# Reordering four token mixers and the cover beside the last one, in a one-core hybrid encoder layer

## The chip, the core and the metric

The kernel runs on one core of one Trainium2 chip. The metric is the device time of the whole program in microseconds (us): the median of three runs. Beside it one execution is profiled, and its instructions, waits and transfers are what this document reads.

## The reference, cut to what matters

One layer of a streaming encoder for 1024 prompt rows and 64 sample rows, width 1024, all in float32:

```python
p = x @ w_in + b_in                       # columns split among four mixers
y = [mLSTM(p), attention(p), HGRN2(p), RG_LRU(p)]     # A, B, C, D, each (t, 512)
mix = sum(sigmoid(x @ w_mg[m] + b_mg[m]) * (y[m] @ w_br[m]) for m in range(4))
x1 = layer_norm(ALPHA * x + mix @ w_out)
x2 = layer_norm(ALPHA * x1 + (gelu(causal_dwconv3(x1 @ w_ff_gate)) * (x1 @ w_ff_up)) @ w_ff_down)
```

The attention needs one forget value per head and row (`log_sigmoid`, then a running sum over the cache and the new rows); the mLSTM needs two gate values per head and row and a running maximum. These are 16 columns of `w_in` in all, the gate rows. The four mixers do not depend on each other: they may run in any order. The states, keys, values and forget logs of both groups are outputs too.

## The kernel before, in words

**Numbers.** A float32 operand is split into a rounded high part and a rest, and a product is three matmuls (high by high, high by rest, rest by high; `mm3`, L305). A weight tile of 128 output columns is loaded by SP (L263), its high part is made by GpSimd for `w_in` (L271) and by ScalarE for all else (L273), its rest by VectorE (L274). `plan` (L199 to L252) lists all weight tiles in the order of use; `wget` issues loads two tiles ahead of use, into two raw and three split buffers.

**Dense tiles.** `dense` (L323) makes one tile of 128 output columns over 1088 rows in three steps (384, 384 and 320 rows), 24 matmuls each. A step is the unit of cover that is woven beside other work. The gate tiles `sigmoid(x @ w_mg)` are stored to DRAM (`th_d`) and read back when the branches are merged. Most of them are made in pairs (`gate_pair`, L503, by `pair`, L373): two tiles with seven products in place of eight over 768 of the rows, fed by sums of weight blocks (`wsums`, L281) and of x blocks (`xsums`, L334). The tiles listed in `PLAIN` (L32) are plain dense tiles: four at the start, while x is being transposed, and tiles 6 and 7 of mixer 0 near the end.

**Order.** The program is written as generators, and `weave(a, na, b, nb)` (L435) runs two of them step by step in the ratio na:nb. `P_X(u)` makes the dense tiles of unit u of mixer X, `M_X(u)` the mixer's own small work (transposes, small matmuls, scans, exponentials). A planner then places the instructions on each engine: work that it takes to be ready may move ahead of work written earlier that is not, by its own estimate of durations; each engine executes its list strictly in that order. DMAs are issued by SP, likewise in order.

The order is D (RG-LRU, 4 units of 6 dense steps), C (HGRN, 4 of 12), B (attention, 4 of 9), A (mLSTM, 2 of 18):

1. Start: `xload`, the bias loads (`pload`, L460; `b_mg`, `ff_conv_w`, `ff_conv_b` and the convolution state go to one tile `pk2r`), transposes of x (`xsplit`), the plain gate tiles of mixer 3. The biases are turned by one transpose (L485), copied (L486), and `bhalf` made from it (L488).
2. 13 gate pairs (L494 to L496).
3. `gate_rows` (L599): 16 columns by a small matmul (L616, L617), through DRAM (`zr_d`, `ls_d`) into a layout with all partitions for the logarithm.
4. `P_D(0)`; then M_D(u) beside P_D(u+1). `fox_rows` (L632: load `ls_d` and the cache's logs, running sums on VectorE, transposes L644 and L657) is chained behind M_D(1); `ml_rows` (L668) behind M_D(3), beside P_C(0).
5. M_C(u) beside P_C(u+1); M_C(3) beside 7 steps of P_B(0), the other 2 steps beside the two tails that M_C leaves (`until_flushed`, L1487).
6. M_B(u) beside P_B(u+1); M_B(3) beside the 18 steps of P_A(0).
7. M_A(0) beside P_A(1). M_A(1) beside 14 steps of a chain: gate tiles 6 and 7 of mixer 0 (6 dense steps), in whose last three steps `ysplit(3, c)` puts the first mixer's result in the place of x; then `merge(3, (0, 2))`, 12 steps of 12 matmuls. Its last four steps stand beside the four tails.
8. `ysplit` of the other mixers and the merges (L766), the output projection, the FFN.

Of the kernel before, what the change touches and what calls it, by code (L numbers as in the profile page):

```python
# [15 lines left out]
OP = mybir.AluOpType  # L16
# [4 lines left out]
P = 128  # L21
# [7 lines left out]
TINY = 1e-30  # L29
ALPHA = 2.0 ** 0.25  # L30
NSLOT = 19
PLAIN = ((3, 0), (3, 2), (0, 6))  # L32
TGRP = ((0, 1, 2), (3, 4, 5), (8, 6, 7))

ML_Q, ML_K, ML_V, ML_O, ML_I, ML_F = 0, 256, 512, 1024, 1536, 1540
# [15 lines left out]
PK_MG = 0  # L51
PK_FW = 32
PK_FB = 80
# [17 lines left out]
def trunk_kernel(ctx: ExitStack, tc: tile.TileContext, I, O, dbg=None):  # L71
# [17 lines left out]
    def phase(s):  # L89
        if temps[0] is not None:  # L90
            temps[0].close()
        temps[0] = ExitStack()
        temps[1] = temps[0].enter_context(tc.tile_pool(name="sp" + s, bufs=3, reuse_waits="tile"))
# [28 lines left out]
    def bank(tag, n=512):  # L122
        return ps1.tile([P, n], F32, tag=tag, name=nm("ps" + tag))
# [80 lines left out]
    def plan_in(c0):  # L204
        plan.append((("in", c0), win(c0), 8))

    def plan_mg(m, e):
        for g in (e, e + 1):
            plan.append((("mg", m, g), I["w_mg"][0, m, :, g * P:g * P + P].rearrange("(k p) c -> p k c", p=P), 8))
# [10 lines left out]
        for c0 in (RG_X, RG_G):  # L220
            plan_in(c0 + u * P)
    for u in range(4):
        for c0 in (HG_F, HG_Q, HG_I, HG_G):
            plan_in(c0 + u * P)
    for u in range(4):
        for c0 in (FX_K, FX_Q, FX_V):
            plan_in(c0 + u * P)
    for u in range(2):
        for c0 in (ML_K + u * P, ML_Q + u * P, ML_V + 2 * u * P, ML_V + 2 * u * P + P,
                   ML_O + 2 * u * P, ML_O + 2 * u * P + P):  # L230
            plan_in(c0)
    plan_mg(0, 6)
    for m in (3, 2, 1, 0):
        for e in (0, 2, 4, 6):
# [191 lines left out]
    def run(*gens):  # L426
        for g in gens:
            for _ in g:
                pass

    def chain(*gens):
        for g in gens:
            yield from g

    def weave(a, na, b, nb):  # L435

        live = [True, True]
        done = [0, 0]
        while live[0] or live[1]:
            i = 0 if live[0] and (not live[1] or done[0] * nb <= done[1] * na) else 1  # L440
            try:
                next((a, b)[i])
                done[i] += 1
            except StopIteration:
                live[i] = False
# [9 lines left out]
    def xload(*tts):  # L455
        for tt in tts:
            xt[tt] = wide["x"].tile([P, D], F32, tag=f"x{tt}", name=nm("xt"), bufs=1) if tt < 8 else slot([P, D], F32, "xt")
            pinned(SP.dma_start(xt[tt][0:tw(tt)], xsrc(tt)))

    def pload(dst, src, raw):  # L460
        n = src.shape[0] // P
        pinned(SP.dma_start(raw[dst:dst + n, :], src.rearrange("(r p) -> r p", p=P)))
# [3 lines left out]
    wissue(0, True)  # L466
    xload(1, 2)
    wissue(1, True)
    for dst, src in ((PK_MG, I["b_mg"][0].rearrange("a b -> (a b)")),
                     (PK_FW, I["ff_conv_w"][0].rearrange("a b -> (a b)")), (PK_FB, I["ff_conv_b"][0]),  # L470
                     (PK1B, I["state_ffn_conv"][0, 0].rearrange("a b -> (a b)"))):
        pload(dst, src, pk2r)
    xload(3, 4, 5, 6, 7, 8)
    for dst, src in ((0, I["b_in"][0, 0:1536]), (12, I["b_in"][0, 1544:3080]), (24, I["b_in"][0, 3088:6160])):
        pload(dst, src, pkb)
    for dst, src in (
# [4 lines left out]
        pload(dst - PK_NG, src, pkr)  # L481
    for tt in range(3):
        xsplit(xt[tt], tt, tt % 2 == 0)
    pt = bank("s", 1024)
    PE.transpose(pt[:, 512:512 + PK2], pk2r[0:PK2, :], ident)  # L485
    V.tensor_copy(pk2, pt[:, 512:512 + PK2])  # L486
    bhalf = const([P, 32], "bhalf")
    V.tensor_scalar(bhalf, pk2[:, PK_MG:PK_MG + 32], 0.5, None, OP.mult)  # L488

    th_d = [[dp.tile([P, T], F32, name=f"th_d{m}_{e}") for e in range(8)] for m in range(4)]  # L490

# [44 lines left out]
    n = PK1 - PK_NG  # L536
    PE.transpose(pt[:, PK_NG:PK1], pkr[0:n, :], ident[0:n, 0:n])
    V.tensor_copy(pk[:, PK_NG:PK1], pt[:, PK_NG:PK1])

    def bc(c0):  # L540
        return pk[:, bcol(c0):bcol(c0) + 1]
# [266 lines left out]
    def P_D(u):  # L808
        xp = slot([P, TP + TS + 6], F32, "xp")
        V.memset(xp[:, 0:3], 0.0)  # L810
        V.tensor_copy(xp[:, TP + 3:TP + 6], pk[:, PK_SC + u:PK_SC + 12:4])
        b = bc(RG_X + u * P)

        def ev(c, n0, n, ps):
            n1 = min(n, TP - n0)
            S.activation(xp[:, 3 + n0:3 + n0 + n1], ps[:, 0:n1], AF.Identity, bias=b)
            if n1 < n:
                S.activation(xp[:, TP + 6:TP + 6 + TS], ps[:, n1:n], AF.Identity, bias=b)
        dx = dense(("in", RG_X + u * P), ev)
        gg = slot(s="gg")  # L820
        bg = bc(RG_G + u * P)

        def ev2(c, n0, n, ps):
            S.activation(gg[:, n0:n0 + n], ps, AF.Identity, bias=bg)
        dg = dense(("in", RG_G + u * P), ev2)
        if u:
            yield from dx
        else:
            for _ in range(2):
                next(dx)  # L830
                yield
                next(dg)
                yield
            next(dx)
            yield
        if u == 0:
            prep_rg()
        uc = slot(s="uc")
        for o, n, _, a in SEG:
            V.tensor_scalar(uc[:, o:o + n], xp[:, a:a + n], pk[:, PK_CW + u:PK_CW + u + 1],  # L840
                            pk[:, PK_CB + u:PK_CB + u + 1], OP.mult, OP.add)
            for j in range(1, 4):
                V.scalar_tensor_tensor(uc[:, o:o + n], xp[:, a + j:a + j + n],
                                       pk[:, PK_CW + 4 * j + u:PK_CW + 4 * j + u + 1],
                                       uc[:, o:o + n], OP.mult, OP.add)
        V.tensor_copy(stD[:, 2:5, u], xp[:, TP:TP + 3])
        V.tensor_copy(stD[:, 5:8, u], xp[:, T + 3:T + 6])
        if u:
            next(dg)
            yield  # L850
        uh = slot(dt=F32R, s="uh")
        S.activation(uh, uc, AF.Copy)
        ul = slot(dt=F32R, s="ul")
        V.tensor_sub(ul, uc, uh.bitcast(F32))
        yield from dg
        st["D", u] = uc, uh, ul, gg

    def M_D(u):
        uc, uh, ul, gg = st.pop(("D", u))
        gates = []  # L860
        for gi, pb in ((0, PK_BA), (1, PK_BX)):
            gt = slot(s="gt")
            for c, (n0, n) in enumerate(CH):
                ps = bank("m")
                mm3(ps[:, :n], [(wab["h"][:, u, gi, :], wab["l"][:, u, gi, :], uh[:, n0:n0 + n], ul[:, n0:n0 + n])])
                S.activation(gt[:, n0:n0 + n], ps[:, :n], AF.Sigmoid, bias=pk[:, pb + u:pb + u + 1])
                yield
            gates.append(gt)
        r, ig = gates
        V.tensor_tensor(ig, ig, uc, OP.mult)  # L870
        tn = slot(s="tn")
        S.activation(tn, r, AF.Tanh, scale=p8[:, u:u + 1])
        S.activation(gg, gg, AF.Gelu_apprx_tanh)
        a = r
        S.activation(a, r, AF.Exp, scale=m8[:, u:u + 1])
        yield
        e2 = slot(s="e2")
        S.activation(e2, a, AF.Square)
        V.scalar_tensor_tensor(e2, e2, 1.0, tn, OP.add, OP.mult)
        V.tensor_scalar(e2, e2, 0.0, None, OP.max)  # L880
        S.activation(e2, e2, AF.Sqrt)
        V.tensor_tensor(e2, e2, ig, OP.mult)
        yield
        h = slot(s="h")
        V.tensor_tensor_scan(h[:, 0:TP], a[:, 0:TP], e2[:, 0:TP], 0.0, OP.mult, OP.add)
        V.tensor_tensor_scan(h[:, TP:T], a[:, TP:T], e2[:, TP:T], pk[:, PK_H0 + u:PK_H0 + u + 1], OP.mult, OP.add)
        V.tensor_copy(stD[:, 0:2, u], h[:, TP - 1:T:TS])
        G.tensor_tensor(gg, h, gg, OP.mult)
        yput(3, u, gg)
        yield  # L890
# [606 lines left out]
    slot_pool(NSLOT)  # L1497
    phase("D")
    gate_rows()
    run(P_D(0))  # L1500
    weave(M_D(0), 10, P_D(1), 6)
    weave(chain(M_D(1), fox_rows()), 13, P_D(2), 6)
    weave(M_D(2), 10, P_D(3), 6)
    weave(chain(M_D(3), ml_rows()), 17, P_C(0), 12)
    out_D()
    phase("C")
    for u in range(1, 4):
        weave(M_C(u - 1), 19, P_C(u), 12)
    g = P_B(0)
    weave(M_C(3), 19, islice(g, 7), 7)  # L1510
    until_flushed(g)
    phase("B")
    for u in range(1, 4):
        weave(M_B(u - 1), 23, P_B(u), 9)
    weave(M_B(3), 23, P_A(0), 18)
    phase("A")
    weave(M_A(0), 21, P_A(1), 18)

    def last_gates():
        for i, _ in enumerate(gates(0, (6, 7))):  # L1520
            if i >= 3:
                xtiles("y", (i - 3,))
                ysplit(3, i - 3)
            yield

    g = chain(last_gates(), merge(3, (0, 2)))
    weave(M_A(1), 21, islice(g, 14), 14)
    until_flushed(g)
    for c in range(3):
        ysplit(2, c)  # L1530
    run(merge(3, (4, 6)))
    for c in range(3):
        ysplit(1, c)
    run(merge(2, (0, 2, 4, 6)))
# [324 lines left out]
```

## Time and profile before

| | us |
|---|---|
| median of 3 runs (lowest, highest) | 2154.87 (2153.61, 2157.75) |
| the profiled execution's own time | 2155.62 |
| span in its profile, first to last instruction | 2153.9 |
| TensorE matmul busy | 2095.9 |
| VectorE busy | 1283.2 |
| ScalarE busy | 791.9 |
| mean granted TensorE clock | 0.991 |

Matmuls are pipelined, so their busy time is not their work; idle time of TensorE and stretches at a lower granted clock are the places to look at. PE is TensorE's matmuls, PEld its weight loads, DVE VectorE, ACT ScalarE, POOL GpSimd, SP SyncE. "A <- B" means that A's engine sat idle until B ended.

### The profile page before, as it was taken

What the parts mean: (1) busy time and instruction counts of PE and PEld (TensorE: products, weight loads), DVE (VectorE), ACT (ScalarE), POOL (GpSimd) and SP (SyncE); (2) the same over time, 40 slices, a digit from 0 to 9 for tenths busy, and PEclk for the clock granted to TensorE, in tenths of its full rate; (3) what the DMA queues carried; (4) which work ended last, traced back from release to release, by engine and by line L of the source; (5) the groups of instructions that cost most, each with busy time, mean ns of one, the idle gap of its engine ahead of it and who ended that gap; (6) DMA issues with size and microseconds to landing.
All of it is one profiled execution on the core that took longest, in us unless ns stands there. A gap on an engine that the chain in (4) does not pass through costs nothing.

```text
span 2153.9 us, 32071 instructions
## 1 busy us (share of the span) xinstructions
PE 2095.9 (97%) x12879; PEld 1939.7 (90%) x12879; DVE 1283.2 (60%) x2438; ACT 791.9 (37%) x1352; POOL 223.9 (10%) x232
## 2 busy tenths in 40 slices
PE   8999999989999999999999999999999999999998
PEld 7999999989988878888999988999889999998886
DVE  6544442556666667556442466767369776666656
ACT  4433332555454424344332342213134333334341
POOL 0000000111211132212101100000130000000112
PEclk9999999999999999999999999999999999999999
DMA  5233233112111122132131156345221223237652
GB/s 165 81 101 102 95 107 97 44 54 62 38 47 44 39 90 65 59 99 81 51 81 41 52 198 175 125 143 179 93 84 51 80 72 89 66 99 280 215 200 103
DMA packets 199856, 212.56 MB, mean 99 GB/s; under 512 B 15324, under 2 KB 170792, under 8 KB 199708
## 3 DMA queue, kind: packets, MB, share of 16 engines
q1 hardware_dynamic: 199708, 210.52, 31.2%
q8 instruction: 101, 1.65, 0.3%
q14 instruction: 47, 0.39, 0.1%
HBM read 160.93 MB, written 49.56 MB: 98 GB/s over the span
## 4 chain that ended last, share of the span: by engine, by line
PE 46%; DVE 3%; DMA 1%; issue 0%; POOL 0%; ACT 0%; DVEq 0%; SPq 0%; ACTq 0%; POOLq 0%
PE pss L386 8%; PE pss L1769 5%; PE psd L308 4%; PE psd L310 4%; PE psd L309 4%; PE psm L308 3%; PE psm L310 3%; PE psm L309 3%; PE psd L1769 2%; PE psm L1769 2%; PE pss L308 1%; PE pss L310 1%; PE pss L309 1%; PE psm L386 1%; PE psm L1385 1%; PE psm L1172 0%
## 5 line engine op out<-in xcount | busy, mean ns | idle before, releaser
L308 PE MATMUL psd<-xh,wh 128*128 128x384 f32 (+1 forms) x1504 | 504.7, 336 | 3.0 <-ACT xh L182 2.6
L310 PE MATMUL psd<-xh,wl 128*128 128x384 f32 (+1 forms) x1504 | 494.2, 329 | 0.0
L309 PE MATMUL psd<-xl,wh 128*128 128x384 f32 (+1 forms) x1504 | 493.5, 328 | 0.4 <-DVE xl L183 0.4
L274 DVE TENSOR_TENSOR wl<-wr,wh 128x1024 fp32r<-128x1024 f32 x179 | 224.3, 1256 | 236.5 <-ACT wh L273 168.4
L308 PEld LDWEIGHTS psd<-xh,wh 128*128 128x128 f32 x1504 | 286.4, 190 | 9.9 <-issue 3.4
L309 PEld LDWEIGHTS psd<-xl,wh 128*128 128x128 f32 x1504 | 285.0, 189 | 1.9 <-DVE xl L183 0.9
L310 PEld LDWEIGHTS psd<-xh,wl 128*128 128x128 f32 x1504 | 285.0, 189 | 0.4
L273 ACT ACTIVATE wh<-wr 128x1024 fp32r<-128x1024 f32 x131 | 138.7, 1059 | 361.1 <-PE psd L309 96.3
L386 PE MATMUL pss<-xs,sh 128*128 128x384 f32 x536 | 136.9, 336 | 0.0
L308 PE MATMUL psm<-yh,wh 128*128 128x384 f32 (+1 forms) x384 | 128.6, 335 | 6.9 <-DVE we L1394 2.7
L271 POOL TENSOR_SCALAR wh<-wr 128x1024 fp32r<-128x1024 f32 x48 | 53.3, 1110 | 770.1 <-PE pss L386 346.1
L309 PE MATMUL psm<-yl,wh 128*128 128x384 f32 (+1 forms) x384 | 127.2, 331 | 0.0
L310 PE MATMUL psm<-yh,wl 128*128 128x384 f32 (+1 forms) x384 | 127.1, 331 | 0.0
L297 DVE TENSOR_TENSOR sl<-st,sh 128x1024 fp32r<-128x1024 f32 x54 | 66.1, 1224 | 51.9 <-ACT sh L296 51.5
L386 PEld LDWEIGHTS pss<-xs,sh 128*128 128x128 f32 x536 | 96.1, 188 | 0.1
L296 ACT ACTIVATE sh<-st 128x1024 fp32r<-128x1024 f32 x54 | 57.3, 1061 | 97.1 <-PE pss L386 44.6
L386 PE MATMUL pss<-xs,sl 128*128 128x384 f32 x268 | 90.0, 336 | 0.0
L1572 POOL TENSOR_TENSOR lrs<-lrs,mhalf 128x1 f32<-128x1 f32 (+1 forms) x16 | 9.8, 614 | 755.9 <-ACT hh L1716 423.9
L1235 DVE CUSTOM_DVE_ANT_0 Pt<-pss,fcb 128x128 f32<-128x128 f32 (+7 forms) x64 | 48.1, 753 | 65.1 <-PE pss L1230 64.6
L308 PE MATMUL psd<-x1h,wh 128*128 128x320 f32 (+1 forms) x272 | 85.3, 313 | 0.6 <-DVE x1l L193 0.6
L310 PE MATMUL psd<-x1h,wl 128*128 128x320 f32 (+1 forms) x272 | 84.9, 312 | 0.0
L309 PE MATMUL psd<-x1l,wh 128*128 128x320 f32 (+1 forms) x272 | 84.8, 312 | 0.0
(556 smaller groups left out, 4530.1 us busy)
## 6 DMA issues: line engine op xcount, KB each, us to landing
wr<-in_w_in_dram SPq DMA_DIRECT2D x48, 512.0 KB
wr<-in_w_ff_down_dram SPq DMA_DIRECT2D x48, 512.0 KB
th_d<-th SPq DMA_DIRECT2D x32, 544.0 KB
th<-th_d SPq DMA_DIRECT2D x32, 544.0 KB
wr<-in_w_mg_dram SPq DMA_DIRECT2D x32, 512.0 KB
wr<-in_w_br_dram SPq DMA_DIRECT2D x16, 512.0 KB
wr<-in_w_ff_gate_dram SPq DMA_DIRECT2D x16, 512.0 KB
wr<-in_w_ff_up_dram SPq DMA_DIRECT2D x16, 512.0 KB
```

Of the source, the lines that this page charges most:

```text
L271: G.tensor_scalar(h, raw, 1.0, 1.0, OP.mult, OP.mult)
L273: S.activation(h, raw, AF.Copy)
L274: V.tensor_sub(l, raw, h.bitcast(F32))
L296: S.activation(h, t, AF.Copy)
L297: V.tensor_sub(l, t, h.bitcast(F32))
L308: PE.matmul(ps, wh, mh, start=i == 0, stop=False)
L309: PE.matmul(ps, wh, ml, start=False, stop=False)
L310: PE.matmul(ps, wl, mh, start=False, stop=i == n - 1)
L386: PE.matmul(ps, w[:, k, :], x[:, k, :], start=start and k == 0 and i == 0, stop=k == 3 and i == 2, skip_group_check=not start)
L1235: V.tensor_tensor_reduce(Pt[:, 0:L].rearrange("p (b n) -> p b n", b=nb), ps.rearrange("p (b n) -> p b n", b=2)[:, 0:nb, 0:n], cbs[hh][:, 0 ...
L1385: PE.matmul(ps[0:w, 0:w], kt[r, t0:t0 + w], qt[r, t0:t0 + w], start=True, stop=True)
L1769: PE.matmul(ps[hf], a[:, f % 8, o:o + P], w[:, 0, sl], start=f == 0 and i == 0, stop=f == 15 and i == (2 if tt < 8 else 1))
```

## The change

The mixers run in the order D, B, C, A. The gate tiles 4 and 5 of mixer 0 leave the pairs (12 pairs are left) and become plain tiles at the end: beside M_A(1) stand 8 steps of four plain gate tiles, the other 4 steps beside the four tails, and the whole of `merge(3, ...)` comes after them. The first part of `fox_rows` (two loads and a running sum) is issued directly behind `gate_rows`, and the rest is woven with P_D(0) after its first two steps; the loads of `ml_rows` are issued before M_B(3), and the rest is chained behind M_B(3), beside P_C(0). M_D(3) stands beside P_B(0), M_C(3) beside 14 steps of P_A(0). At the start `b_mg` is loaded alone into a tile of 32 rows ahead of the later x tiles and turned alone; the three other vectors are loaded behind x and turned later, before the pairs.

```diff
@@ -29,7 +29,7 @@
 TINY = 1e-30
 ALPHA = 2.0 ** 0.25
 NSLOT = 19
-PLAIN = ((3, 0), (3, 2), (0, 6))
+PLAIN = ((3, 0), (3, 2), (0, 4), (0, 6))
 TGRP = ((0, 1, 2), (3, 4, 5), (8, 6, 7))
 
 ML_Q, ML_K, ML_V, ML_O, ML_I, ML_F = 0, 256, 512, 1024, 1536, 1540
@@ -220,15 +220,16 @@
         for c0 in (RG_X, RG_G):
             plan_in(c0 + u * P)
     for u in range(4):
-        for c0 in (HG_F, HG_Q, HG_I, HG_G):
+        for c0 in (FX_K, FX_Q, FX_V):
             plan_in(c0 + u * P)
     for u in range(4):
-        for c0 in (FX_K, FX_Q, FX_V):
+        for c0 in (HG_F, HG_Q, HG_I, HG_G):
             plan_in(c0 + u * P)
     for u in range(2):
         for c0 in (ML_K + u * P, ML_Q + u * P, ML_V + 2 * u * P, ML_V + 2 * u * P + P,
                    ML_O + 2 * u * P, ML_O + 2 * u * P + P):
             plan_in(c0)
+    plan_mg(0, 4)
     plan_mg(0, 6)
     for m in (3, 2, 1, 0):
         for e in (0, 2, 4, 6):
@@ -466,11 +467,12 @@
     wissue(0, True)
     xload(1, 2)
     wissue(1, True)
-    for dst, src in ((PK_MG, I["b_mg"][0].rearrange("a b -> (a b)")),
-                     (PK_FW, I["ff_conv_w"][0].rearrange("a b -> (a b)")), (PK_FB, I["ff_conv_b"][0]),
+    pkm = small([32, P], "trif", 1)
+    pload(0, I["b_mg"][0].rearrange("a b -> (a b)"), pkm)
+    xload(3, 4, 5, 6, 7, 8)
+    for dst, src in ((PK_FW, I["ff_conv_w"][0].rearrange("a b -> (a b)")), (PK_FB, I["ff_conv_b"][0]),
                      (PK1B, I["state_ffn_conv"][0, 0].rearrange("a b -> (a b)"))):
-        pload(dst, src, pk2r)
-    xload(3, 4, 5, 6, 7, 8)
+        pload(dst - PK_FW, src, pk2r)
     for dst, src in ((0, I["b_in"][0, 0:1536]), (12, I["b_in"][0, 1544:3080]), (24, I["b_in"][0, 3088:6160])):
         pload(dst, src, pkb)
     for dst, src in (
@@ -481,11 +483,10 @@
         pload(dst - PK_NG, src, pkr)
     for tt in range(3):
         xsplit(xt[tt], tt, tt % 2 == 0)
-    pt = bank("s", 1024)
-    PE.transpose(pt[:, 512:512 + PK2], pk2r[0:PK2, :], ident)
-    V.tensor_copy(pk2, pt[:, 512:512 + PK2])
+    pt = bank("m")
+    PE.transpose(pt[:, 0:32], pkm, ident[0:32, 0:32])
     bhalf = const([P, 32], "bhalf")
-    V.tensor_scalar(bhalf, pk2[:, PK_MG:PK_MG + 32], 0.5, None, OP.mult)
+    V.tensor_scalar(bhalf, pt[:, 0:32], 0.5, None, OP.mult)
 
     th_d = [[dp.tile([P, T], F32, name=f"th_d{m}_{e}") for e in range(8)] for m in range(4)]
 
@@ -536,6 +537,9 @@
     n = PK1 - PK_NG
     PE.transpose(pt[:, PK_NG:PK1], pkr[0:n, :], ident[0:n, 0:n])
     V.tensor_copy(pk[:, PK_NG:PK1], pt[:, PK_NG:PK1])
+    n = PK2 - PK_FW
+    PE.transpose(pt[:, 512:512 + n], pk2r[0:n, :], ident[0:n, 0:n])
+    V.tensor_copy(pk2[:, PK_FW:PK2], pt[:, 512:512 + n])
 
     def bc(c0):
         return pk[:, bcol(c0):bcol(c0) + 1]
@@ -1497,38 +1501,43 @@
     slot_pool(NSLOT)
     phase("D")
     gate_rows()
-    run(P_D(0))
-    weave(M_D(0), 10, P_D(1), 6)
-    weave(chain(M_D(1), fox_rows()), 13, P_D(2), 6)
-    weave(M_D(2), 10, P_D(3), 6)
-    weave(chain(M_D(3), ml_rows()), 17, P_C(0), 12)
+    fox = fox_rows()
+    next(fox)
+    g = P_D(0)
+    run(islice(g, 2))
+    weave(fox, 3, g, 4)
+    for u in range(1, 4):
+        weave(M_D(u - 1), 10, P_D(u), 6)
+    weave(M_D(3), 10, P_B(0), 9)
     out_D()
+    phase("B")
+    for u in range(1, 4):
+        weave(M_B(u - 1), 23, P_B(u), 9)
+    ml = ml_rows()
+    next(ml)
+    weave(chain(M_B(3), ml), 29, P_C(0), 12)
     phase("C")
     for u in range(1, 4):
         weave(M_C(u - 1), 19, P_C(u), 12)
-    g = P_B(0)
-    weave(M_C(3), 19, islice(g, 7), 7)
+    g = P_A(0)
+    weave(M_C(3), 19, islice(g, 14), 14)
     until_flushed(g)
-    phase("B")
-    for u in range(1, 4):
-        weave(M_B(u - 1), 23, P_B(u), 9)
-    weave(M_B(3), 23, P_A(0), 18)
     phase("A")
     weave(M_A(0), 21, P_A(1), 18)
 
     def last_gates():
-        for i, _ in enumerate(gates(0, (6, 7))):
-            if i >= 3:
-                xtiles("y", (i - 3,))
-                ysplit(3, i - 3)
+        for i, _ in enumerate(gates(0, (4, 5, 6, 7))):
+            if i >= 9:
+                xtiles("y", (i - 9,))
+                ysplit(3, i - 9)
             yield
 
-    g = chain(last_gates(), merge(3, (0, 2)))
-    weave(M_A(1), 21, islice(g, 14), 14)
+    g = last_gates()
+    weave(M_A(1), 21, islice(g, 8), 8)
     until_flushed(g)
     for c in range(3):
         ysplit(2, c)
-    run(merge(3, (4, 6)))
+    run(merge(3, (0, 2, 4, 6)))
     for c in range(3):
         ysplit(1, c)
     run(merge(2, (0, 2, 4, 6)))
```

## Rows read from the trace of the kernel before

**Rows 1.** The page, busy time of each engine over the span
```profile
PE 2095.9 (97%) x12879; PEld 1939.7 (90%) x12879; DVE 1283.2 (60%) x2438; ACT 791.9 (37%) x1352; POOL 223.9 (10%) x232
```

**Rows 2.** Waits of TensorE, whole span: us in total, times, longest us
```profile
PE psm L1012 <- DVE vt L1016: 8.3, 5, 3.1
...
PE psm L644 <- DMA clf<-in_cache_fox_logf_dram: 4.3, 1, 4.3
PE pss L1225 <- DVE mn L1235: 3.7, 3, 1.2
PE psm L308 <- DVE we L1394: 2.7, 4, 1.2
...
PE psm L308 <- DVE th L782: 2.3, 2, 1.9
PE psm L714 <- DVE mli L684: 2.2, 1, 2.2
PE psm L1459 <- DVE mnum L1449: 2.2, 1, 2.2
PE psm L308 <- ACT zn L1463: 1.9, 3, 0.8
```

**Rows 3.** Windows on granted clock: start:end length, busy us (x instructions), PEclk, DMA
```profile
460.45:470.69 10.24, 8.66 (x35) 7.25 (x34) 2.80 (x6) 7.47 (x11) 0.00 (x0) 0.50 0.10 10
532.13:535.54 3.41, 3.41 (x13) 2.97 (x12) 2.73 (x9) 1.01 (x1) 0.00 (x0) 0.50 0.25 71
757.41:764.23 6.82, 5.76 (x22) 5.53 (x22) 6.33 (x8) 1.20 (x2) 3.86 (x3) 0.50 0.29 79
1317.19:1320.60 3.41, 3.41 (x13) 3.13 (x13) 0.75 (x2) 0.38 (x1) 0.00 (x0) 0.50 1.37 96
```

**Rows 4.** Windows by stage, same columns: M_C(1), M_C(3), M_A(0), M_A(1)
```profile
608.60:674.10 65.50, 63.62 (x445) 58.11 (x445) 41.83 (x78) 30.00 (x66) 11.77 (x9) 1.00 0.16 45
...
739.70:800.70 61.00, 56.49 (x384) 48.18 (x382) 40.92 (x80) 16.76 (x52) 16.96 (x13) 0.94 0.22 67
...
1140.90:1237.60 96.70, 96.70 (x606) 87.94 (x606) 38.63 (x150) 23.98 (x60) 11.57 (x13) 1.00 0.15 46
1237.60:1322.90 85.30, 77.76 (x466) 67.39 (x464) 60.25 (x228) 32.59 (x74) 7.91 (x9) 0.96 0.66 183
```

**Rows 5.** Window over pairs, line L386 alone: PE, PEld, PEclk, DMA
```profile
90.77:311.38 220.61, 153.59 (x842) 145.36 (x842) 1.00 0.30 99
```

**Rows 6.** Window over one plain dense tile, all engines
```profile
408.49:420.32 11.83, 11.83 (x74) 11.83 (x73) 9.57 (x14) 7.43 (x9) 0.18 (x1) 1.00 0.17 46
```

**Rows 7.** Timeline of SP (issues): start us, us, line, out<-in
```profile
378.29 0.32 SPq L620 DMA_DIRECT2D zr_d<-z  x1
380.23 0.36 SPq L623 DMA_DIRECT2D zz<-zr_d  x1
387.40 0.34 SPq L630 DMA_DIRECT2D ls_d<-zll  x1
391.72 0.39 SPq L263 DMA_DIRECT2D wr<-in_w_in_dram  x1
...
437.24 13.43 SPq L263 DMA_DIRECT2D wr<-in_w_in_dram  x2
450.77 0.42 SPq L634 DMA_DIRECT2D fx<-ls_d  x1
...
456.89 0.43 SPq L638 DMA_DIRECT2D clf<-in_cache_fox_logf_dram  x1
```

**Rows 8.** Timeline of TensorE at the cache's forget logs: start us, us, [idle before <-releaser]
```profile
459.82 1.31 PE L644 MATMUL psm<-ident,clf 128*8 128x128 f32 x8 [4.29 <-DMA clf<-in_cache_fox_logf_dram]
```

**Rows 9.** Groups of VectorE in the window of M_A(1): busy us, mean ns, idle before
```profile
L747 DVE TENSOR_TENSOR yl<-yr,yh 128x768 fp32r<-128x768 f32 (+1 forms) x12 | 10.7, 902 | 1.0 <-ACT yh L746 1.0
...
L782 DVE SCALAR_TENSOR_TENSOR th<-th,psm 128x384 f32<-128x384 f32 (+1 forms) x12 | 6.4, 531 | 3.8 <-PE psm L310 3.7
```

**Rows 10.** Timeline of TensorE at the start
```profile
12.42 0.45 PE L485 MATMUL pss<-ident,pk2r 128*128 128x128 f32 x1 [0.46 <-DMA pk2r<-in_state_ffn_conv_dram]
14.59 1.26 PE L308 MATMUL psd<-xh,wh 128*128 128x384 f32 x2 [1.72 <-ACT xh L182]
```

## The prediction, made before the changed kernel was run

> **What bounds the kernel now.** I read the page first, for which engine is full: TensorE, 97% busy [rows 1], which leaves 2153.9 - 2095.9 = 58.0 us of idle time. Next the waits of TensorE, for where that idle time is: beside the start, nearly all of it lies in the mixers, and not where the dense tiles run but where a mixer's small work has too little dense work beside it [rows 2]. [...] At half the clock a matmul does half, so a stretch costs half its length. Last the windows by stage, to see what a unit costs over its dense steps [rows 4]. VectorE at 60% and ScalarE at 37% have room on the whole; POOL and the DMAs matter only where a wait names them.
>
> So the time is TensorE's work plus its stalls, and an edit is worth what it does to either.
>
> **The change part by part.** *Pair to plain.* The window over pairs holds 842 matmuls of L386, 84 to a pair, so 10 pairs in 220.61 us: 22.06 us each [rows 5]. Two plain tiles take 2 x 11.83 = 23.66 us [rows 6], so a step is 3.94 us. The trade costs **+1.6 us** of TensorE's work. The two weight splits move with the tiles, and one pair's block sums go from VectorE and ScalarE, which have room at either place; without it the splits would show as waits for `wh` or `wl`, which rows 2 do not have.
>
> *Forget rows.* Now SP issues the load of `ls_d` at 450.77 and, in order behind it, that of the cache's logs only at 456.89 [rows 7]; TensorE idles 4.29 us until they land at 459.82 [rows 8] and then runs 10.24 us at half clock [rows 3]. Together 4.3 + 5.1 = 9.4 us. After the change both loads stand behind `gate_rows`. A DMA that waits for an earlier one's landing is issued 380.23 - 378.29 = 1.94 us after it [rows 7], so `ls_d`, stored at 387.40, is loaded from 389.3, the logs are issued at 389.8 and land 2.93 us later (456.89 to 459.82), at 392.7. TensorE is past the small matmul by 378.3 and has the four steps of P_D(0) that are left, 15.8 us, to 394.1: enough, if the planner puts the transposes behind them. Behind the waiting load on SP stands the next weight load, which went out at 391.72 anyway [rows 7], so the wait holds nothing back. [...] On VectorE, behind the running sum, stand the convolution of P_D(0) and so M_D(0), which P_D(1) covers. I take -9.4 + 1.5 for a wait somewhere near the new place: **-7.9**, bounds -9.4 and the first rival's price.
>
> *mLSTM rows.* The wait at L714 is 2.2 us [rows 2], its clock 3.41 / 2 = 1.7 [rows 3]: 3.9 us. Their three loads move ahead of M_B(3), where SP's queue is the loads of the attention; the running sums then need no load, and VectorE can do them while M_B(3) runs. The transposes still follow the sums, with only 2 to 3 dense steps woven beside them. I take **-2.9**, bounds -3.9 and 0.
>
> *M_B(3) with 12 steps and the rows, not 18.* M_B(0) to M_B(2) have 9 steps beside them and wait 1.2 us each at L1225, three times in all; M_B(3) with 18 does not wait there [rows 2]. **+1.2**, bounds 0 and 1.2. P_B(0) moves beside M_D(3) with the same instructions and DMAs; nothing is late for it.
>
> *M_C(3).* M_C(1) takes 65.5 us with 12 steps, 65.5 - 47.3 = 18.2 of its own; M_C(3) takes 61.0 with 9, 25.5 of its own, of which about 1 us is P_B's transposes: 6.3 us too much [rows 4]. The rows name it: the longest of the five waits at L1012 is 3.1 where the other four average (8.3 - 3.1) / 4 = 1.3 [rows 2], and half of 6.82 us of low clock [rows 3], 5.2 together. With 14 steps of P_A(0) it should be as M_C(1). **-4.5**, bounds -6.3 and 0.
>
> *M_A(1).* M_A(0) takes 96.7 - 18 x 3.94 = 25.8 us of its own; M_A(1) takes 85.3 - 6 x 3.94 - 12 x 1.97 = 38.0 [rows 4]. Of the 12.2 us more, the waits on L1394, L1449 and L1463 are 6.8 [rows 2] and two clock stretches 3.4. The cover is the same in sum, 47.3 us, but 15.8 of it instead of 7.9 now stand beside the four tails, where the 2.2 us wait for the last normalisation is, and 31.5 instead of 39.4 beside the unit itself. Against the thinner cover, VectorE loses 10.7 us of `ysplit` and 6.4 us of merging in that stretch [rows 9], about a quarter of its 60.25 us [rows 4], and those delays are what TensorE waited for. I take half, **-6.0**; bounds -12.2 and 0.
>
> *The seam to the merges.* `merge(3)` now follows the last gate tile at once, and its y must be split in the place of x: chunk 2 can only start when that tile is done, two splits of 0.9 us on VectorE [rows 9] and as much on ScalarE before them, against two merge steps (3.9 us) that run meanwhile. **+1.5**, bounds 0 and 3. The wait of 1.9 us for `th` in the later merges [rows 2] is in text that is not touched; I leave it.
>
> *Start.* The transpose of the biases waits 0.46 us for the last vector, but TensorE then waits 1.72 us for x's split on ScalarE [rows 10]: **0**, bounds -0.5 and +0.5. The later transposes of the other vectors are one matmul and one copy more. That x is issued three DMAs earlier helps nothing that waits.
>
> Sum: 1.6 - 7.9 - 2.9 + 1.2 - 4.5 - 6.0 + 1.5 = **-17.0 us**. Against the profiled execution's own 2155.62 that is 2138.6; that execution lies 0.75 above the median of the runs, so I say **2138 us**. With every term at its good end, 1.6 - 9.4 - 3.9 - 6.3 - 12.2 - 0.5 = -30.7: 2124.
>
> **The rivals.** *Half of it* (20%): the stalls that rows name as single late loads go (-7.9 and -2.9), but M_C(3) and M_A(1) are bound by their own chains of small instructions, and more or other cover changes nothing: -17.0 + 4.5 + 6.0 = -6.5, about 2148. For it: M_A(1) has thinner cover ahead of its tails. Against it: M_C(1) and M_A(0) run with cover and without these waits [rows 4].
>
> *The stall only moves* (8%): the change does not do what it says, since the planner puts the transposes where they are written, right behind the small matmul. TensorE waits from 378.3 to 392.7, 14.4 us, and pays up to 5.1 for the clock: 19.5 in place of 9.4. The sum becomes -17.0 + 7.9 + 10.1 = +1.0: 2156, no change. Against it: planned order goes by readiness, and the chain of four DMAs is known to the planner.
>
> *The loads queue behind a weight load* (9%): on SP a weight load that waits for a buffer holds all behind it, 13.43 us over two issues ahead of the load of `ls_d` now [rows 7]. If the planner places one ahead of the cache's logs again, they come 13.4 us later, at 406.1. TensorE, with four steps to 394.1, waits 12.0 us; with the transposes placed ahead of those steps, 27.8. The second, with 5.1 for the clock, is 32.9 in place of 9.4: -17.0 + 7.9 + 23.5 = +14.4, about 2169, slower. With the other terms as above the change loses from a wait of some 13 us on. Against it: SP had nothing to issue between 387.40 and 391.72 [rows 7]. [...]
>
> *All of it* (10%): every term near its good end, about 2128.
>
> **How the numbers follow.** The forecast of 2138 has 53%. 0.2% of the time, 4.3 us, is what a measurement of this kernel can tell from no change. Faster by more, under 2150.6: the forecast, "all of it", and three quarters of "half of it": 0.78. Within 0.2%: the rest of that and most of "only moves": 0.12. Slower: the queue and the rest: 0.10. The range runs from 2126, near the good ends, to 2155, which takes in "half of it" and the lower edge of "only moves"; about 2 in 10 lie outside.
>
> **What would show it.** Right: no wait at L644 over 1 us and no half clock near it; the logs issued right behind the load of `ls_d`; the longest wait at L1012 under 2 us; no wait at L1459; M_C(3) and M_A(1) within a few us of their sisters after taking off 3.94 us a step; 12 pairs of 22.06 us. Wrong: a wait at L644 between 378 and 400 us; new waits at the first merge on `yh` or `yl` beyond 3 us; or a waiting weight split where the order of weights has changed. The prediction as a whole fails if idle time of TensorE in the mixers does not fall by some 10 us.

## The result and the profile after

The changed kernel takes 2172.23 us (median of 4 runs, 2170.60 to 2174.95) where the kernel before, run beside it, takes 2155.03: a ratio of 1.008, 95% interval 1.0062 to 1.0097. It is slower by some 17 us; 2138 was forecast, with the range ending at 2155. Line numbers of after are mostly 1 to 4 higher (L644 is L648, L1012 is L1016, L782 is L786).

TensorE's busy time on the page, which answers to [rows 1], went from 2095.9 to 2099.2 us:

```profile
PE 2099.2 (97%) x12892; PEld 1942.1 (90%) x12892; DVE 1276.6 (59%) x2428; ACT 789.1 (36%) x1348; POOL 220.6 (10%) x232
```

So 12.7 us more lie in idle time (70.7 against 58.0). Windows cut the span at three instructions that both kernels have: the last matmul of the gate rows, the last L1385/L1389 of M_A(0), the last matmul of the merges. Columns are start:end, length, then busy us (x instructions) of PE, PEld, DVE, ACT and POOL, granted clock, DMA share and GB/s. Before:

```profile
0.00:377.05 377.05, 366.23 (x2176) 354.71 (x2177) 176.72 (x279) 142.27 (x211) 7.56 (x20) 1.00 0.33 107
377.05:1226.80 849.75, 823.44 (x5703) 749.12 (x5702) 491.72 (x1004) 355.01 (x711) 150.61 (x164) 0.99 0.21 59
1226.80:1493.40 266.60, 257.18 (x1548) 245.48 (x1549) 182.04 (x464) 72.60 (x140) 13.69 (x14) 0.98 0.50 154
```

After, with M_C(3), M_A(1) and the two longest stretches at the granted 0.50 (answering to [rows 3, 4]):

```profile
0.00:355.48 355.48, 344.35 (x2044) 333.03 (x2044) 167.27 (x263) 132.63 (x197) 6.53 (x19) 1.00 0.33 106
355.48:1212.90 857.42, 823.71 (x5702) 748.86 (x5702) 490.88 (x1008) 355.93 (x713) 148.68 (x165) 0.99 0.21 59
1212.90:1509.10 296.20, 281.86 (x1692) 269.71 (x1693) 186.05 (x466) 78.44 (x148) 13.45 (x14) 0.97 0.45 147
...
1032.50:1127.10 94.60, 91.86 (x610) 84.33 (x609) 42.58 (x86) 22.36 (x64) 18.60 (x17) 0.98 0.20 61
...
1223.80:1303.00 79.20, 76.72 (x465) 66.86 (x463) 45.32 (x205) 26.93 (x68) 7.67 (x9) 0.98 0.31 88
358.94:376.01 17.07, 7.67 (x26) 6.61 (x27) 8.00 (x14) 4.95 (x9) 0.00 (x0) 0.50 0.07 13
1311.26:1324.91 13.65, 5.79 (x20) 5.82 (x21) 6.21 (x9) 3.95 (x5) 0.00 (x0) 0.50 1.02 373
```

The first stretch is 21.57 us shorter: the pair that left. The middle, with the same matmuls, is 7.7 us longer. The end is 29.6 us longer; two plain tiles are 23.66 of that, so 5.9 are loss. What follows the merges is equal within 0.3. The waits of TensorE (us in total, times, longest us) name both losses; compare [rows 2]:

```profile
PE psm L309 <- DVE th L786: 11.3, 2, 10.5
PE psd L309 <- ACT xp L820: 8.0, 1, 8.0
PE psm L1016 <- DVE vt L1020: 5.6, 3, 2.1
PE psm L648 <- DMA clf<-in_cache_fox_logf_dram: 4.7, 1, 4.7
...
PE psm L898 <- DVE stD L891: 2.8, 1, 2.8
...
PE pss L1229 <- DVE mn L1239: 2.5, 2, 1.2
PE psm L1016 <- DVE gs L1033: 2.5, 1, 2.5
PE psm L1463 <- DVE vr L1448: 2.0, 1, 2.0
```

**Stall one, at the gate rows.** ScalarE's timeline (start, us, engine, line, operation; in brackets the idle time before and its releaser), then TensorE's:

```profile
355.66 0.52 ACT L622 ACTIVATE z<-psm,b 16x320 f32<-16x320 f32 x1 [1.75 <-PE psm L621]
360.69 0.32 ACT L629 ACTIVATE zu<-zz 128x136 f32<-128x136 f32 x1 [4.51 <-DMA zz<-zr_d]
...
362.66 0.32 ACT L551 ACTIVATE lpzl<-lpzw 128x136 f32<-128x136 f32 x1
363.00 0.58 ACT L820 ACTIVATE xp<-psd,pk 128x384 f32<-128x384 f32 x1
363.48 0.57 ACT L828 ACTIVATE gg<-psd,pk 128x384 f32<-128x384 f32 x1
```

```profile
363.64 0.69 PE L309 MATMUL psd<-xh,wh 128*128 128x384 f32 x1 [8.02 <-ACT xp L820]
364.12 0.52 PE L310 MATMUL psd<-xl,wh 128*128 128x384 f32 x1
364.44 0.52 PE L311 MATMUL psd<-xh,wl 128*128 128x384 f32 x1
364.76 0.52 PE L309 MATMUL psd<-xh,wh 128*128 128x384 f32 x1
365.08 0.52 PE L310 MATMUL psd<-xl,wh 128*128 128x384 f32 x1
370.31 1.01 PE L648 MATMUL psm<-ident,clf 128*8 128x128 f32 x4 [4.71 <-DMA clf<-in_cache_fox_logf_dram]
```

The first two dense steps of P_D(0) had run and filled both banks `psd`. Their evictions (L820, L828) stand on ScalarE behind the logarithm of the gate rows, which waits for `zz` to come back from DRAM; ScalarE sits idle for 4.51 us with two full banks. TensorE's third step can't start. Five matmuls of it later stand the transposes, and the cache's logs have not landed. The place of these transposes would have held TensorE just as long by itself: it works through its list in order (the 19 dense matmuls that stand behind L648 in this step need no logs, and the first of them starts at 371.83) and the logs are there at 370.31, so with prompt evictions it would have stood at L648 from about 356.5 on (an estimate: five matmuls, 0.17 us each, behind the last one of the gate rows at 355.62). The late evictions fill the first 8.0 us of a wait that the logs end.

**Stall two, at the first merge.** SP's issues, and VectorE at the same place:

```profile
1305.90 6.14 SPq L747 DMA_DIRECT2D yr<-y_d  x12
1312.53 1.93 SPq L776 DMA_DIRECT2D th<-th_d  x4
```

```profile
1315.04 2.58 DVE L751 TENSOR_TENSOR yl<-yr,yh 128x768 fp32r<-128x768 f32 x3 [0.15 <-ACT yh L750]
1318.42 1.02 DVE L786 SCALAR_TENSOR_TENSOR th<-th,psm 128x384 f32<-128x384 f32 x2 [0.80 <-DMA th<-th_d]
```

`ysplit(2)` is now written ahead of all of `merge(3)`, so its 12 loads are issued ahead of the first `th` loads, and the DMAs are full (share 1.02, 373 GB/s) in the stretch up to 1324.9. `th` lands 5.9 us after its issue, and TensorE waits 10.49 us with full banks. On VectorE, six splits of the second y (L751) stand ahead of the first L786; the last of them ends at 1317.62, and VectorE then waits 0.80 us for `th`. As the lists stand, `th` on time would have freed the banks only 0.8 us earlier: the late loads and the early splits hold TensorE over the same time.

### The profile page after: what moved, and what is told of

It reads as the page before. It is cut to its first block, busy times and chain, and to the rows that moved or that the text cites. A ratio compares the mean times of both kernels' runs of the same rounds, so it can differ in the third digit from the quotient of the medians.

```text
span 2169.9 us, 32059 instructions
## 1 busy us (share of the span) xinstructions
PE 2099.2 (97%) x12892; PEld 1942.1 (90%) x12892; DVE 1276.6 (59%) x2428; ACT 789.1 (36%) x1348; POOL 220.6 (10%) x232
## 4 chain that ended last, share of the span: by engine, by line
PE 81%; DVE 10%; issue 4%; DMA 3%; ACT 1%; POOL 1%; SPq 0%; DVEq 0%; POOLq 0%; ACTq 0%
PE pss L387 15%; PE psd L309 11%; PE psd L311 11%; PE psd L310 11%; PE pss L1778 4%; PE psm L309 3%; PE psm L310 3%; PE psm L311 3%; PE psm L387 2%; PE psm L1778 2%; PE psd L1778 2%; PE pss L309 1%; PE pss L311 1%; PE pss L310 1%; DVE wl L275 1%
## 5 line engine op out<-in xcount | busy, mean ns | idle before, releaser
L309 PE MATMUL psd<-xh,wh 128*128 128x384 f32 (+1 forms) x1536 | 517.4, 337 | 9.0 <-ACT xp L820 8.0
L311 PE MATMUL psd<-xh,wl 128*128 128x384 f32 (+1 forms) x1536 | 507.1, 330 | 0.0
L310 PE MATMUL psd<-xl,wh 128*128 128x384 f32 (+1 forms) x1536 | 505.0, 329 | 0.6 <-DVE xl L183 0.6
L309 PEld LDWEIGHTS psd<-xh,wh 128*128 128x128 f32 x1536 | 293.5, 191 | 16.3 <-ACT xp L820 8.3
L310 PEld LDWEIGHTS psd<-xl,wh 128*128 128x128 f32 x1536 | 291.8, 190 | 2.4 <-DVE xl L183 1.1
L311 PEld LDWEIGHTS psd<-xh,wl 128*128 128x128 f32 x1536 | 292.0, 190 | 1.0 <-issue 0.5
L309 PE MATMUL psm<-yh,wh 128*128 128x384 f32 (+1 forms) x384 | 127.1, 331 | 11.8 <-DVE th L786 11.3
L387 PE MATMUL pss<-xs,sh 128*128 128x384 f32 x512 | 130.8, 336 | 0.0
L309 PEld LDWEIGHTS psm<-yh,wh 128*128 128x128 f32 x384 | 73.0, 190 | 12.9 <-issue 11.8
```

The costliest lines, as they stand in the source:

```text
L309: PE.matmul(ps, wh, mh, start=i == 0, stop=False)
L310: PE.matmul(ps, wh, ml, start=False, stop=False)
L311: PE.matmul(ps, wl, mh, start=False, stop=i == n - 1)
L387: PE.matmul(ps, w[:, k, :], x[:, k, :], start=start and k == 0 and i == 0, stop=k == 3 and i == 2, skip_group_check=not start)
```

## The experiments

Each kernel was timed beside runs of the kernel before, on the same chip; ratios are to it. A (8.0 + 4.7 us of waiting) is stall one, B (10.5) is stall two.

**1. The forget rows back.**
```diff
-    fox = fox_rows(); next(fox); g = P_D(0); run(islice(g, 2)); weave(fox, 3, g, 4)
+    run(P_D(0)); ... weave(chain(M_D(1), fox_rows()), 13, P_D(2), 6)
```


> The changed kernel with the forget rows back behind M_D(1), where the kernel before has them; all else as changed. Theory (the early forget rows stall TensorE twice, by 8.0 and 4.7 us, and cost half the clock for 17.07 us, about 21 us, where the old place cost 9.4): these stalls go, a wait of some 4 us at the transposes of clf beside P_D(2) returns with some 10 us of half clock: 2172 - 11.5 = about 2161. Rival (the stalls belong to gate_rows with a thin P_D(0), or to the new order of mixers, not to the forget rows): the wait of 8 us at P_D(0)'s third step stays, and the time is about 2172 or above it.

2166.56 us, ratio 1.0055 (1.004 to 1.0069). A is gone, and the old wait is back (4.35 us, with half clock from 436.0). So the early forget rows make A; but the gain is 5.7, half of the 11.5 expected. What I had priced too high is the low clock: 17.07 us of it at A, yet TensorE is busy in 7.67 of them only. The wait itself lies in the stretch and is not doubled by it. By half the busy time, A costs 8.0 + 4.7 + 3.8 = 16.6 and the old place 4.3 + 8.66 / 2 = 8.6 [rows 3, 8]: 8.0 apart, which the intervals of the two ratios allow.

**2. The first part written two steps later, 3. and then `prep_rg` ahead of it.**
```diff
-    next(fox)
     g = P_D(0)
     run(islice(g, 2))
+    next(fox)
```


> The changed kernel with one line moved: the first part of fox_rows is written behind the first two steps of P_D(0) instead of ahead of them, so P_D(0) takes its buffers first. Theory (buffers are handed out in the order written; behind fx8, cr and clf, xp and gg come late, their evictions stand on ScalarE behind the logarithm of the gate rows, and TensorE fills both banks and waits): the evictions of P_D(0) come before the logarithm, the wait of 8.0 us is under 1, and the transposes of clf move some 120 matmuls later, where the load has landed or is 1 to 4 us short: 2172 - 21 = 2151 with no wait there, 2159 with 4 us and its half clock. Rival (an early running sum and its loads are what costs, wherever the buffers are taken): 2168 to 2172, with a wait of 8 us or more still between 350 and 380 us.

2173.37 us, ratio 1.0091 (1.0075 to 1.0107). ScalarE's first two evictions now come ahead of the logarithm, and the transposes stand some 130 dense matmuls behind the gate rows and wait 0.63 us for `clf`: A is gone, as the theory says. The one line moved both, so this run doesn't tell the evictions' part from that of the transposes' place. The time is not better, since another wait was behind it. ScalarE, SP (first what it waited for: us in total, times, longest us; then its issues), VectorE and TensorE in this run:

```profile
351.61 0.58 ACT L820 ACTIVATE xp<-psd,pk 128x384 f32<-128x384 f32 x1
352.09 0.57 ACT L828 ACTIVATE gg<-psd,pk 128x384 f32<-128x384 f32 x1
...
361.01 0.32 ACT L629 ACTIVATE zu<-zz 128x136 f32<-128x136 f32 x1
```

```profile
SPq L665 <- DVE fo L664: 7.8, 1, 7.8
```

```profile
382.34 0.38 SPq L665 DMA_DIRECT2D out_dram<-fo  x1
...
385.81 1.27 SPq L802 DMA_DIRECT2D wabr<-in_rg_w_x_dram  x2
...
390.12 1.23 DVE L807 TENSOR_TENSOR wabl<-wabr,wabh 128x1024 fp32r<-128x1024 f32 x1 [7.49 <-POOL wabh L805]
391.26 1.03 DVE L844 TENSOR_SCALAR uc<-xp,pk 128x1024 f32<-128x1024 f32 x2
...
397.70 0.98 PE L309 MATMUL psm<-uh,wabh 128*128 128x384 f32 x2 [15.38 <-issue]
```

`wabr`, the block-diagonal weights, are written last in P_D(0). Their loads, which need nothing but a buffer and a memset, went out at 383.5 to 387.1 us: on SP they stood behind the stores of the forget rows, and SP waited 7.8 us for `fo` before the first of these (L665). The split of `wabr` on VectorE (L807) stood ahead of the convolution (L844). (The profile puts TensorE's wait down to "issue"; VectorE's rows tell what it was.) Run 3 moves them:

```diff
     def P_D(u):
+        if u == 0:
+            prep_rg()
         xp = ...
```


> The run with the forget rows behind two steps of P_D(0) (2173.4), and the block-diagonal weights of RG-LRU (prep_rg) taken first in P_D(0), ahead of the forget rows. Theory (in that run wabr took its buffers last, its loads went out at 383 to 387 us, the convolution stood behind its split on VectorE until 391.3, and TensorE waited 15.38 us for uh with 17.07 us at half clock): the loads go out near 345 us, that wait falls under 2 us, no half clock near it: 2173.4 - 15.4 - 8.5 = 2149.5, so 2148 to 2152. Rival (the convolution is late because the two running sums and the copies of the forget rows stand ahead of it on VectorE): wabr comes early and TensorE still waits 5 us or more for uh: 2156 or more.

2163.80 us, ratio 1.004 (1.0026 to 1.0054), 9.6 better than run 2 and still far from 2150. The loads go out at 346.8, and the wait for `uh` falls to 3.40 us with 6.83 us of half clock, 5.75 of them busy. The rival has part of it: on VectorE the two running sums (2.28 us each) now stand right ahead of the convolution. Most of the rest of my miss is the clock, priced as in run 1: by half the busy time run 2's wait cost 15.38 + 5.95 / 2 = 18.4 us and this one costs 3.40 + 5.75 / 2 = 6.3. These are 12.1 apart, which the intervals of the two ratios allow for the 9.6 measured. Together the two runs say that A is a matter of the order in which things are written. For `wabr` one channel is on record, SP's in-order queue. That buffers, which are asked for in the order of writing, are another was my theory; no run shows it apart, and how the planner comes to its lists stays open.

**4, 5. The seam: the splits behind the first two pairs of `merge(3)`, or the `th` loads ahead of the splits.**
```diff
+    run(merge(3, (0, 2)))
     for c in range(3):
         ysplit(2, c)
-    run(merge(3, (0, 2, 4, 6)))
+    run(merge(3, (4, 6)))
```


> The changed kernel with the splits of the second mixer's y written behind the first two pairs of merge(3), as in the kernel before. Theory (the 12 loads of yr stand on SP ahead of the first th loads, which come 6 us late; TensorE waits 10.5 us and runs 13.65 us at half clock, 17 together): the th loads are issued some 6 us earlier, the wait is under 4 us, the time about 2172 - 14 = 2158. Rival (TensorE waits there for the split of the first mixer's y into the place of x, or th_d itself is late): the wait at the first merge stays at 8 us or more, with yh or yl as releaser, and the time is within 4 us of 2172.

> The changed kernel with the splits where they are, but the first four th loads of merge(3) issued ahead of them. The order of loads on SP is then that of the run with the late splits, while VectorE and ScalarE still do the splits of the second mixer early. If SP's order alone makes the stall: as that run, about 2158, within 4 us of it. If the splits on VectorE and ScalarE ahead of the merges' own work cost as well: a wait of 3 us or more at the merges with th or yl as releaser, and the time between 2160 and 2170.

2163.94 us (1.003 to 1.006) and 2166.20 (1.0037 to 1.0072): 8.3 and 6.0 better than the change where 14 was expected, and not to be told apart. So the splits written ahead of the merges make B. Through which queue the two runs don't show. Run 5 was to keep the splits early on VectorE and ScalarE, and they did not stay so: on VectorE the first split of the second y starts at 1322.02, behind five L789 (L786 of the change), as in run 4, where it starts at 1320.07. SP's order and VectorE's moved together in both runs. And TensorE's idle time at the seam doesn't vanish; in run 4 it reads:

```profile
1305.11 0.69 PE L309 MATMUL psm<-yh,wh 128*128 128x384 f32 x1 [4.39 <-ACT zn L1467]
1313.40 0.38 PE L309 MATMUL psm<-yh,wh 128*128 128x320 f32 x1 [1.08 <-DVE th L786]
```

**6. The old end under the new order.** `PLAIN`, the last gate tiles and `merge(3, (0, 2))` in the chain beside M_A(1) as before.

> The changed kernel with the end of the kernel before: 13 pairs, two plain gate tiles beside M_A(1), merge(3, (0, 2)) in the chain beside it; mixers' order, forget rows and mLSTM rows as changed. Theory (the new end wins 6 us in M_A(1), pays 1.6 for the pair and 17 for the th loads behind the yr loads): 2172.2 - 17 - 1.6 + 6.1 = about 2160, near the run with the late splits (2163.9) or some us below. Rival (the seam costs what it does because attention and HGRN have changed places, so that another y is split there): the wait at the merges stays above 8 us and the time above 2168.

2160.95 us, ratio 1.0027 (1.0016 to 1.0039), as expected: the change's end costs 11.3 us (by the windows above 5.9 and 1.6 for the pair, within the intervals).

**7. The old end and the forget rows behind all of P_D(0).**
```diff
+    run(P_D(0))
+    fox = fox_rows()
+    next(fox)
+    weave(chain(fox, M_D(0)), 13, P_D(1), 6)
```


> The end of the kernel before, the changed order of mixers and mLSTM rows, and the forget rows written behind the whole of P_D(0): loads and running sum directly behind it, the rest ahead of M_D(0) beside P_D(1). Theory (all stalls that the change brought come from the order in which buffers and loads were written, and its gains are real): no wait above 2 us between 350 and 400 us, no wait above 2 us at the transposes of clf: 2160 - 21 = about 2139, and faster than the kernel before by some 15. Rival (a load of the cache's logs behind a weight load on SP is late wherever it stands): a wait of 4 us or more at the transposes of clf, with half clock, and 2147 to 2150.

2145.86 us, ratio 0.9956 (0.9943 to 0.9968): faster than the kernel before. A is gone, 15.1 us against run 6 by one edit, close to its 16.6 less what is left:

```profile
PE psm L897 <- DVE stD L890: 2.8, 1, 2.8
...
PE psm L647 <- DMA clf<-in_cache_fox_logf_dram: 1.7, 1, 1.7
```

The expected 2139 was again too good by the price of the clock, and by the 1.7 us left. The rival, a load late behind a weight load, shows 1.7 us and no half clock.

**8. The kernel before with that edit alone.**

> The kernel before with the forget rows alone moved, written behind the whole of P_D(0) as in the run above; order of mixers, mLSTM rows and end as before. Theory (the old place costs 4.3 us of waiting and 5.1 of half clock, and the early place is free if the buffers of P_D(0) are taken first): the wait at L644 is gone, 2154 - 9.4 = about 2144.5. Rival (the wait and its half clock only move, to the transposes or to uh ahead of M_D(0)): within 3 us of 2154.

2146.84 us, ratio 0.9959 (0.9945 to 0.9974): -8.2 of the expected -9.4, with 1.8 us of waiting left. The early place is a gain, in the right order of writing. All else in run 7, the order of the mixers, the mLSTM rows and the start, makes the difference of 1.0 us between the two runs, which their intervals don't tell from nothing.

**9. The change's own end with both repairs (runs 4 and 7 together).**

> The changed kernel with its own end (12 pairs, four plain gate tiles, all of merge(3) behind them) and both repairs: forget rows behind the whole of P_D(0), and the splits of the second y behind the first two pairs of merge(3). Against the run with the old end (2145.9) it shows what the new end is worth once nothing stands ahead of the th loads. Theory (6 us won in M_A(1), 1.6 paid for the pair, and at the seam a wait of 4 us for zn with some 3.4 of half clock, as in the run with the late splits alone): within 3 us of 2145.9, more likely above, about 2148. Rival (the new end is a gain of 4 us or more, as forecast): 2142 or less.

2149.66 us, ratio 0.9974 (0.9963 to 0.9984), 3.8 above run 7. Last stretch of the span, run 7 and then run 9:

```profile
1218.90:1483.20 264.30, 254.49 (x1548) 242.91 (x1549) 181.73 (x464) 72.69 (x140) 13.69 (x14) 0.99 0.50 156
```

```profile
1198.90:1488.30 289.40, 278.42 (x1693) 266.95 (x1693) 185.32 (x466) 78.00 (x148) 13.42 (x14) 0.99 0.46 150
```

Idle time of TensorE is 264.30 - 254.49 = 9.8 us with the old end and 289.40 - 278.42 = 11.0 with the new one. What M_A(1) wins by its better cover comes back where the merges, without M_A(1) beside them, wait for `zn` and `th` (3.5 and 5.0 us in run 9).

**10. `out_D` behind M_B(0).** Run 7 with `out_D()` moved one unit back, its tile a slot.

> The run with the old end and the repaired forget rows (2145.9), with out_D written behind M_B(0) instead of directly behind M_D(3), and its small tile taken as a slot. Theory (TensorE waits 2.81 us for the last column of stD because M_D(3) ends with nothing left beside it): that wait goes and nothing takes its place, 2145.9 - 2.8 - up to 1.7 of half clock = 2142 to 2143. Rival (the wait only covers time that M_B(0) would wait for its own exponentials): within 1.5 us of 2145.9.

2142.75 us, ratio 0.9945 (0.9932 to 0.9957), 3.1 below run 7. The wait for `stD` is gone, and the waits at L1228 have grown from 2.5 to 4.0 us. The 3.1 is not clear of noise: the two intervals overlap, and the two profiled executions have spans of 2143.5 and 2143.7. It is the lowest median of all, 12 us below the kernel before.

**11. The old start under run 7.**

> The run with the old end and the repaired forget rows (2145.9), with the start of the kernel before: all four vectors loaded together and turned at once. Theory (the start is bound by x's loads, and the changed start costs or gives nothing on average): within 1.5 us of 2145.9. Rival (the biases' own load, whose transpose waits 1.2 to 3.2 us in the runs with the new start against 0.46 in the kernel before, costs that): 2144 or less.

2146.51 us (0.9949 to 0.9974), 0.65 above run 7: no difference. The biases' transpose waits longer in the new start (2.1 us in run 7, 0.46 in the kernel before [rows 10]), and TensorE waits less for x's split on ScalarE (0.9 us over the whole span in run 7, 2.6 in the kernel before).

**12. The mLSTM loads not issued ahead, under run 7.**
```diff
-    ml = ml_rows(); next(ml)
-    weave(chain(M_B(3), ml), 29, P_C(0), 12)
+    weave(chain(M_B(3), ml_rows()), 29, P_C(0), 12)
```


> The run with the old end and the repaired forget rows (2145.9), with the loads of the mLSTM rows no longer written ahead of M_B(3) but with the rest of the rows behind it. Theory (the early loads let the running sums go beside M_B(3) and so end the wait of 2.2 us and its 3.41 us of half clock): both return, 2145.9 + 3 = about 2149. Rival (the wait is gone because the rows stand behind M_B(3) with P_C(0) still whole, whenever they are loaded): the wait at mli stays under 1 us and the time within 1.5 us of 2145.9.

2148.70 us (0.9965 to 0.9984), 2.8 above run 7, all ten executions above run 7's five: the theory's size, and not its place. No wait returns at `mli`; the running sum starts at 831.40 in place of 826.74, and what stands behind the rows on VectorE, M_C(0), is late instead:

```profile
866.54 0.30 PE L1015 MATMUL psm<-ident,vT 128*64 128x128 f32 x1 [4.72 <-DVE vt L1019]
```

## Why the prediction was wrong

| Step | Forecast | Measured | From |
|---|---|---|---|
| pair to plain | +1.6 | +1.6 | pairs as long as before |
| forget rows | -7.9 | +8.0 | 16.6 for 8.6 by rows; run 1 measured 5.7 |
| mLSTM rows | -2.9 | -2.8 | run 12, the early loads alone |
| M_B(3) | +1.2 | -1.2 | two waits at L1229 for three |
| `out_D`, M_D(3) | 0 | +2.8 | wait at L898; 3.1 in run 10, not clear of noise |
| M_C(3) | -4.5 | -1.8 | 94.60 - 18 x 3.94 = 23.7 for 25.5 |
| M_A(1) | -6.0 | -6.1 | 79.20 - 12 x 3.94 = 31.9 for 38.0 |
| seam | +1.5 | +12.0 | end of +5.9 in all, plus 6.1 |
| start | 0 | +0.5 | 22.06 - 21.57 |

The sum is 13.0 of the 16.0 us between the spans (2169.9 and 2153.9); 3 us of the middle are in no row of mine.

**The forget rows** fell at "enough, if the planner puts the transposes behind them". The chain of loads was right: `ls_d` is issued 10.5 us after the small matmul, and the logs land 4.3 us behind it (5.3 said). But the condition failed and the four dense steps were no cover: the transposes stand five matmuls into the first of them, and TensorE stood 8.0 + 4.7 us until the logs had landed. Nor could those steps have run on: I followed the early rows along SP and TensorE and never along ScalarE, where evictions of P_D(0) stand behind the logarithm. The trace has 4.51 us of idle ScalarE there, ahead of two evictions that could run. "The stall only moves", with its 8%, came closest: the transposes near where they are written, and 19.5 us in place of 9.4, against 16.6 in place of 8.6. It did not have the evictions, and it came to 2156 because it kept every other term as forecast. Which of the two, evictions or transposes, the planner would have had to place otherwise stays open.

**The seam** fell at "+1.5, bounds 0 and 3". I counted the splits of the first y, and left out that `ysplit(2)` moves ahead of all of `merge(3)`: 12 DMAs past four `th` loads on SP, and six splits past the first L786 on VectorE. How the 12.0 divides between the two stays open. The rival "the loads queue behind a weight load" gave 2169 and the mechanism of a queue on SP, at the wrong place: the cache's logs were issued at 367.97, right behind `fx` at 367.64. That its 2169 lies near the 2172 measured is luck: it had +23.5 at the forget rows, where +8.0 was found, and nothing of the seam.

**M_A(1)** came out as forecast in size, though its sign "no wait at L1459" was not met: 2.0 us are left there (L1463), now for `vr` and not for `mnum`. It was still no gain: bounding a stage by its own window hid that its idle time moves on to the merges (run 9). Of the "two clock stretches" of this stage before, [rows 3] show the second; the first is:

```profile
1283.06:1286.47 3.41, 3.19 (x12) 3.20 (x13) 2.06 (x10) 2.51 (x4) 1.01 (x1) 0.50 0.15 49
```

**M_C(3)** won 1.8 of the 4.5: one wait of 2.5 us at L1016 and 3.41 us of half clock are left where 3.1 and 6.82 were, so the longer cover took away a part only.

**The clock** was mis-sized throughout by "a stretch costs half its length". Half of the busy time in it is about what a stretch costs: within stall one, at the granted 0.50, matmuls that follow each other start 0.32 us apart (364.12, 364.44, 364.76), and at the granted 1.00 the same matmuls start 0.17 apart (343.98, 344.15, 344.32), while idle time in the stretch is a wait that is counted already. For the old place that is 8.6, not 9.4; for A 3.8, not 8.5. The runs side with half the busy time: run 7 won 15.1 us, where A less the 1.7 us left is 14.9 by half the busy time and 19.6 by my price.

**`out_D`** was the step costed at nothing without naming its cover: P_C(0) with 12 steps stood beside M_D(3) and the rows behind it, P_B(0) has 9 and they are used up.

## What to carry to other kernels

Before writing a step earlier, list what it is written ahead of on every queue and in every pool of buffers, and follow the longest round trip in it to whatever stands behind on an in-order engine: an eviction there stops TensorE as surely as a late operand (here 8.0 us and 4.7 us in the change). Write an early load behind the buffers and loads of the work that is meant to cover it. A stage that gains cover has won only when the idle time of the whole stretch up to the next full stage has fallen.

## What the runs showed that was not expected

A stretch at the granted 0.50 may hold little work: 7.67 us busy of 17.07, 5.79 of 13.65, and 5.95 of 17.07 in run 2, against 8.66 of 10.24 before. And at a seam the order of loads is felt: 12 loads of `yr` (2.2 MB by their shapes, an estimated 6 us at the 373 GB/s measured) put the `th` loads back by about that, their 6.14 us of issuing.
